# Loading the second attention's first query weights before the last rows of the first feed-forward are transposed

## The chip, the cores and the metric

The kernel runs on one core of one Trainium2 chip. The metric is device time in microseconds (us) of one execution, and the median of three executions is given. Five engines work side by side: TensorE (PE; its weight loads appear as PEld), VectorE (DVE), ScalarE (ACT), GpSimd (POOL) and SyncE (SP), which here issues nearly all transfers between the chip's main memory and its on-chip memory. Each engine works through its own instructions in order; semaphores hold an instruction back until what it needs is there.

## The reference

A trunk of two layers works on a sequence of 1024 rows of 1024 numbers. The first layer mixes rows with latent attention, the second with differential attention. A normalisation follows each mixer, then a gated feed-forward and a normalisation. The place of the change is the seam between the first layer's feed-forward and the second layer's mixer:

```python
def _swiglu(x, w_gu, w_down):
    gate, up = jnp.split(x @ w_gu, 2, axis=-1)
    return (jax.nn.silu(gate) * up) @ w_down

def _diff_mixer(x, w_in, ...):
    h = x @ w_in
    q, k, v = jnp.split(h, [qk_w, 2 * qk_w], axis=-1)
    ...

for i in range(DEPTH):
    ...
    h = _layernorm(ALPHA * h + mix, ln_mix_g[i], ln_mix_b[i])
    h = _layernorm(ALPHA * h + _swiglu(h, ffn_w_gu[i], ffn_w_down[i]), ln_ffn_g[i], ln_ffn_b[i])
```

## The kernel before

Every float32 product is made of three products of rounded parts: an operand is split into a high part (ACT casts it, line 519 or 136) and a low part (the operand less its high part, line 520 or 137, on DVE or POOL), and TensorE adds high by high, high by low and low by high.

The feed-forward's down projection saves multiplications by combining blocks of its operands (the h side and the w side) before the products. Its last product, called t4 here, runs over 11 steps j = 0 to 10. For each step an h block is split (tile op_h, low part on DVE) and a w block is built and split: DVE subtracts (line 865, rw_t less tt), ACT casts (op_w_t), POOL subtracts for the low part. Then TensorE adds twelve 128x512 matmuls into four banks named dw (line 889). The blocks come in three loads each: rh holds the h blocks, rw_t the w blocks of steps 0-3, 4-7 and 8-10. There are two buffers for rh, so the third rh load, and behind it on SP the third rw_t load, is asked for when the first rh block has been used up by step 3.

This is how TensorE takes one step of t4 (its order, step 3, with the engines that it waits for; the numbers behind the tiles are buffer numbers):

```order
L889 MATMUL dw_0_9091<-op_w_t_3_9877,op_h_4_3_9873 128x512 [waits Activation_49]
L889 MATMUL dw_1_9092<-op_w_t_3_9877,op_h_4_3_9873 128x512
L889 MATMUL dw_2_9093<-op_w_t_3_9877,op_h_4_3_9873 128x512
L889 MATMUL dw_3_9094<-op_w_t_3_9877,op_h_4_3_9873 128x512
L889 MATMUL dw_0_9091<-op_w_t_3_9877,op_h_4_3_9873 128x512 [waits Pool_49]
L889 MATMUL dw_0_9091<-op_w_t_3_9877,op_h_4_3_9873 128x512 [waits DVE_49]
L889 MATMUL dw_1_9092<-op_w_t_3_9877,op_h_4_3_9873 128x512 x2
```

Four matmuls need high parts alone, the fifth needs POOL's low part of w, the sixth DVE's low part of h. This stands the same before and after the change.

After t4 the rows are normalised (`layer_norm`): DVE centres a row block (line 176), ACT squares it (line 170), POOL takes a power (line 181, tile rs_f), DVE scales (line 184), and TensorE transposes it (line 148, tile xTp_f). The second mixer's first products follow: values (tile bv, weights wbv) and, for head 0, queries (tile bp, weights wb0_0).

`load_w` loads one weight block and splits it; it is where the change acts:

```python
raw = wp.tile([P, 1024], F32, tag="wr", bufs=2, name=f"r_{name}")
nc.sync.dma_start(raw[:, :cols], src)                                        # line 132
hi = wp.tile([P, 1024], F32R, tag="wh", name=f"h_{name}")
lo = wp.tile([P, 1024], F32R, tag="wl", name=f"l_{name}")
A.copy(hi[:, :cols], raw[:, :cols])                                          # line 136
j = (eng or G).tensor_tensor(lo[:, :cols], raw[:, :cols], f32(hi[:, :cols]), ALU.subtract)   # 137
```

The raw buffers (tag wr) are two and are taken in turn. `next_x` runs when the stage t4 has been written down and loads the value weights; `proj_b` loads query and key weights when a head first asks for them. `behind(i, j)` puts instruction i behind j in the order, without a semaphore. The order on each engine is set at build time by a scheduler with priorities, so where an instruction is written does not alone say where it stands.

Of the kernel before, what the change touches and what calls it, by code (L numbers as in the profile page):

```python
# [42 lines left out]
def trunk(  # L43
# [63 lines left out]
    def f32(t):  # L107
        return t.bitcast(F32)
# [7 lines left out]
    def ps_m(name):  # L116
        return ps.tile([P, 512], F32, tag="m", bufs=ps_bufs[1], name=name)
# [10 lines left out]
    def load_w(src, cols, name, hi=None, lo=None, eng=None, raw=None, ins=False):  # L128

        if raw is None:  # L130
            raw = wp.tile([P, 1024], F32, tag="wr", bufs=2, name=f"r_{name}")
        nc.sync.dma_start(raw[:, :cols], src)
        if hi is None:
            hi = wp.tile([P, 1024], F32R, tag="wh", name=f"h_{name}")
            lo = wp.tile([P, 1024], F32R, tag="wl", name=f"l_{name}")
        A.copy(hi[:, :cols], raw[:, :cols])
        j = (eng or G).tensor_tensor(lo[:, :cols], raw[:, :cols], f32(hi[:, :cols]), ALU.subtract)
        return (hi, lo, j.ins) if ins else (hi, lo)

    def mm3(ps_out, pairs):  # L140
        n = len(pairs)
        for i, (lh, ll, rh, rl) in enumerate(pairs):
            T.matmul(ps_out, lh, rh, start=(i == 0), stop=False)  # L143
            T.matmul(ps_out, lh, rl, start=False, stop=False)  # L144
            T.matmul(ps_out, ll, rh, start=False, stop=(i == n - 1))  # L145
# [9 lines left out]
    def behind(i, j):  # L155

        tc.add_manual_dep(
            i, j.name,
            mybir.DependencyInfo(mybir.DependencyClass.NoSync, mybir.DependencyReason.DATA),
            reason="kept in program order",  # L160
        )
# [38 lines left out]
    def new_xT(pool, name):  # L200
        t = {
            (p, hf): pool.tile([P, KD, 512], F32R, tag=f"xT{p}{hf}", name=f"xT{p}{hf}_{name}")
            for hf in range(2) for p in range(2)
        }
        return [[t[p, hf] for hf in range(2)] for p in range(2)]
# [327 lines left out]
    def swap(side):  # L533
        return "left" if side == "right" else "right"

    def ffn(side, xo, xst, pending, layer, x_src, x_dst, lng, lnb, next_x, spare=()):


# [494 lines left out]
        else:  # L1033
# [3 lines left out]
            whole(y4, from_h(2, "4", ("o",)), t4(), False)  # L1037
            stx.close()
            new = next_x()
            with tc.high_priority(60):  # L1040
                for t in range(4, 8):
# [169 lines left out]
    with ast as st:  # L1211
# [6 lines left out]
        vt, qr, qn, kn, wts, lt, pts = {}, {}, {}, {}, {}, {}, {}  # L1218
# [125 lines left out]
    xst, wts = ExitStack(), {}  # L1344

    def next_x():
        pool = xst.enter_context(tc.tile_pool(name="xp0", bufs=1, side="right", reuse_waits="tile"))
        wts["v", 0] = [load_w(w_b_v[0, kh], 1024, f"wbv0_{kh}") for kh in range(2)]
        return new_xT(pool, "f0")

    xo, stacks = x_pools("m0", "right")
# [2 lines left out]
    def split_wo(h, c):  # L1354

        cs = slice(c * 512, c * 512 + 512)
        raw = wp.tile([P, 1024], F32, tag="wr", name=f"pwo{h}_{c}", bufs=2)[:, :512]
        nc.sync.dma_start(raw, w_o_b[h][:, cs])
        nc.sync.dma_start(wo_dr[h][:, :, cs], f32(op_unit(raw, V, f"pwo{h}_{c}")))

    xT, rest, normed = ffn(
        "left", xo, stacks, pending, 0, xs_dr[0], xs_dr[1], ln_ffn_g[0], ln_ffn_b[0], next_x,
        [lambda h=h, c=c: split_wo(h, c) for h in range(H) for c in range(2)],
    )
# [3 lines left out]
    with ExitStack() as st:  # L1368
# [11 lines left out]
        for ql in q_lo:  # L1380
            for mp in range(2):
                b = slice(64 - mp * 64, 128 - mp * 64)
                z = bb[b, :512]
                i = G.tensor_tensor(ql[b, mp * 512:mp * 512 + 512], z, z, ALU.subtract).ins
# [20 lines left out]

        def proj_b(h, which, hf):
            if (which, h) not in wts:
                *wts[which, h], i = load_w(w_b_qk[h, which], 1024, f"wb{h}_{which}", ins=True)
                if len(wts) == 2:
                    behind(i, normed[0][2])  # L1410
            wh, wl = wts[which, h]
            hs = slice(hf * 512, hf * 512 + 512)
            m = ps_m(f"bp{h}_{which}_{hf}")
            mm3(m, [(wh[:, k * P:k * P + P], wl[:, k * P:k * P + P], xT[0][hf][:, k, :], xT[1][hf][:, k, :])
                    for k in range(KD)])
            sc = float(2.0 ** (h + 1) / 8.0)
            if which == 0:
                j = 2 * h + (hf if h < H - 1 else 1 - hf)
                q2, ql = q_slot[h, hf] = q_hi[j % 3], q_lo[j % 3]
                for mp in range(2):  # L1420
                    a = slice(mp * 64, mp * 64 + 64)
                    b = slice(64 - mp * 64, 128 - mp * 64)
                    qh = q2[:, mp * 512:mp * 512 + 512]
                    A.activation(qh[a], m[a, :], AF.Copy, scale=sc)
                    V.scalar_tensor_tensor(
                        ql[a, mp * 512:mp * 512 + 512], m[a, :], sc, f32(qh[a]), ALU.mult, ALU.subtract
                    )
                    nc.gpsimd.dma_start(qh[b], qh[a])
            else:
                for mp in range(2):  # L1430
                    a = slice(mp * 64, mp * 64 + 64)
                    b = slice(64 - mp * 64, 128 - mp * 64)
                    k = kt[h % 2][:, mp]
                    A.copy(k[a, hs], m[a, :])
                    V.tensor_tensor(k[b, hs], m[a, :], f32(k[a, hs]), ALU.subtract)
# [74 lines left out]
        at(-1, first_values)  # L1510
        at(-1, rest[0])
        at(-1, proj_b, 0, 0, 1)
        for tb in range(4):
            for fn in rest[tb + 1:tb + 2]:
                at(-1, fn)
            at(-1, values_b, 0, tb)
        at(-1, proj_b, 0, 0, 0)
        at(-1, proj_b, 0, 1, 0)
        at(-1, proj_b, 0, 1, 1)
        at(-1, table)  # L1520
# [128 lines left out]
```

## Time and profile before

| what | us |
|---|---|
| median of 3 executions | 2256.71 |
| lowest and highest | 2256.47 and 2257.42 |
| the profiled execution | 2256.85 |
| its span in the trace | 2255.1 |
| TensorE busy in the span | 2235.1 |

The profile is of one execution. The span runs from the first to the last instruction, and the profiled execution's own time is 1.75 us longer. Times in the timelines count from the start of the span. In a timeline row the first number is the start, the second the time from the first start to the last end of the merged instructions, `x3` their count, and the bracket at the end says how long the engine was idle before and what ended that.

### The profile page before, as it was taken

How to read it: one execution, taken by the hardware profiler on the slowest of the kernel's cores; microseconds unless marked ns; L12 is line 12 of the kernel's file. 1: busy time of each engine (PE TensorE's matmuls, PEld its weight loads, DVE VectorE, ACT ScalarE, POOL GpSimd, SP SyncE). 2: the span in 40 equal slices, each digit the busy share in tenths (PEclk: the TensorE clock that was granted, in tenths of full speed). 3: DMA queues.
4: the chain of work that ended last, by engine and by line, in shares of the span. 5: the costliest groups of instructions: out<-in, count | busy, mean ns of one | idle time of the engine just before them, and what ended most of it. 6: DMA issues, size and time to landing. Idle time of an engine off the chain costs nothing.

```text
span 2255.1 us, 31061 instructions
## 1 busy us (share of the span) xinstructions
PE 2235.1 (99%) x11410; PEld 1911.9 (85%) x11410; DVE 1543.9 (68%) x2894; ACT 1014.0 (45%) x2097; POOL 773.5 (34%) x626
## 2 busy tenths in 40 slices
PE   9999999999999999999999999999999999999998
PEld 8899998888888888888989898988888888888886
DVE  5676765696666657767576666577787656658778
ACT  4455664352333334444465656455432333334444
POOL 2232341114434440456432424222014444430551
PEclk9999999999999999999999999999999999999999
DMA  5010125334535338454310212063344232238453
GB/s 204 14 35 32 42 71 187 141 130 146 181 126 201 121 131 327 177 201 150 103 44 32 64 34 68 24 224 131 121 148 163 82 110 101 102 112 331 160 183 149
DMA packets 105545, 287.76 MB, mean 128 GB/s; under 512 B 7968, under 2 KB 30112, under 8 KB 94896
## 3 DMA queue, kind: packets, MB, share of 16 engines
q1 hardware_dynamic: 101552, 277.44, 34.6%
q0 software_dynamic: 3840, 8.33, 1.4%
q8 instruction: 90, 1.47, 0.3%
q14 instruction: 63, 0.52, 0.1%
HBM read 204.47 MB, written 77.07 MB: 125 GB/s over the span
## 4 chain that ended last, share of the span: by engine, by line
PE 96%; DVE 2%; DMA 1%; ACT 1%; issue 1%; POOL 0%; SPq 0%; DVEq 0%; POOLq 0%; ACTq 0%
PE gb L563 16%; PE gc L563 11%; PE ga L563 10%; PE dw L889 8%; PE dx L889 5%; PE zp_a L431 4%; PE s_a L220 3%; PE s_b L220 3%; PE dv L889 3%; PE dy L889 3%; PE bp L145 3%; PE bp L143 3%; PE bp L144 3%; PE o_a L263 2%; PE o_b L263 2%; PE hq L1142 2%
## 5 line engine op out<-in xcount | busy, mean ns | idle before, releaser
L519 ACT CAST op_g<-gr 128x512 fp32r<-128x512 f32 x240 | 146.8, 621 | 377.9 <-PE gb L563 185.8
L520 POOL TENSOR_TENSOR op_g<-gr,op_g 128x512 fp32r<-128x512 f32 x104 | 144.9, 1398 | 253.8 <-ACT op_g L519 141.6
L520 DVE TENSOR_TENSOR op_h<-rh,op_h 128x512 fp32r<-128x512 f32 x152 | 140.1, 948 | 51.1 <-ACT op_h L519 51.1
L563 PE MATMUL ga<-xh_m,op_g 128*128 128x512 f32 x512 | 168.2, 389 | 0.0
L889 PE MATMUL dw<-op_w_t,op_h 128*128 128x512 f32 x660 | 151.2, 390 | 0.0
L519 ACT CAST op_h<-rh 128x512 fp32r<-128x512 f32 x152 | 91.9, 619 | 124.3 <-PE dx L889 32.6
L889 PEld LDWEIGHTS dw<-op_w_t,op_h 128*128 128x128 f32 x660 | 123.6, 188 | 25.8 <-DVE op_h L520 0.3
L228 ACT ACTIVATE l_b<-l_b,mx_b 128x256 f32<-128x256 f32 (+7 forms) x128 | 99.4, 777 | 74.8 <-DVE mx_b L223 72.9
L520 DVE TENSOR_TENSOR op_g<-gr,op_g 128x512 fp32r<-128x512 f32 x136 | 112.9, 833 | 17.1 <-ACT op_g L519 16.8
L520 POOL TENSOR_TENSOR op_w_b<-rw_b,op_w_b 128x512 fp32r<-128x512 f32 x44 | 64.7, 1493 | 172.1 <-ACT op_w_b L519 172.0
L1451 POOL TENSOR_SCALAR l_b<-l_b,rb,cst 128x128 f32<-128x128 f32 (+3 forms) x64 | 52.5, 821 | 200.5 <-DVE rb L1450 188.0
L889 PE MATMUL dx<-op_w_b,op_h 128*128 128x512 f32 x528 | 120.3, 389 | 0.0
L889 PEld LDWEIGHTS dx<-op_w_b,op_h 128*128 128x128 f32 x528 | 99.1, 188 | 20.6
L563 PE MATMUL gb<-t2h_f,op_g 128*128 128x512 f32 x352 | 115.4, 390 | 0.4 <-DVE op_g L520 0.4
L563 PE MATMUL gc<-t1h_f,op_g 128*128 128x512 f32 x352 | 115.6, 389 | 0.0
L563 PE MATMUL gb<-t4h_f,op_g 128*128 128x512 f32 x352 | 115.5, 389 | 0.0
L563 PE MATMUL gc<-b22h_f,op_g 128*128 128x512 f32 x352 | 115.4, 389 | 0.0
L563 PE MATMUL gb<-t3h_f,op_g 128*128 128x512 f32 x352 | 115.2, 389 | 0.0
L563 PEld LDWEIGHTS ga<-xh_m,op_g 128*128 128x128 f32 x512 | 96.1, 188 | 19.9
L520 POOL TENSOR_TENSOR op_g<-s,op_g 128x512 fp32r<-128x512 f32 x40 | 55.2, 1381 | 166.5 <-ACT op_g L519 158.6
L143 PE MATMUL bp<-xT_f,h_wb 128*128 128x512 f32 x256 | 101.8, 398 | 0.0
L144 PE MATMUL bp<-xT_f,h_wb 128*128 128x512 f32 x256 | 101.6, 397 | 0.0
(389 smaller groups left out, 6689.5 us busy)
## 6 DMA issues: line engine op xcount, KB each, us to landing
gr<-in_w_gu SPq DMA_DIRECT2D x44, 1024.0 KB, 6.8
rh<-h_dr SPq DMA_DIRECT2D x28, 1024.0 KB, 4.8
h_dr<-sh SPq DMA_DIRECT2D x22, 1024.0 KB, 5.0
h_dr<-hp SPq DMA_DIRECT2D x22, 768.0 KB, 4.1
tt<-in_w_dn SPq DMA_DIRECT2D x22, 512.0 KB, 8.8
rh<-h_dr SPq DMA_DIRECT2D x12, 768.0 KB, 4.4
wo_dr<-op_pwo SPq DMA_DIRECT2D x16, 512.0 KB, 3.3
z<-xs_dr SPq DMA_DIRECT2D x16, 512.0 KB, 11.1
```

Of the source, the lines that this page charges most:

```text
L143: T.matmul(ps_out, lh, rh, start=(i == 0), stop=False)
L144: T.matmul(ps_out, lh, rl, start=False, stop=False)
L145: T.matmul(ps_out, ll, rh, start=False, stop=(i == n - 1))
L220: T.matmul(s[:, :w], lh, rh[:, ks], start=(j == 0), stop=(j == len(q_pass) - 1))
L228: ends["exp"] = A.activation(l[:, :n], l[:, :n], AF.Exp, bias=mx, scale=-1.0, accum_out=sm).ins
L263: T.matmul(po[:, c], a, b[:, j % 2, c], start=st, stop=sp_, skip_group_check=True)
L431: T.matmul(m, a[:, h, :], self.wo[h][w][:, c], start=(start and h == heads[0] and a is oh and w == 0), stop=(stop and h == heads[-1] and a ...
L519: turns["cast"] = A.copy(hi, src).ins
L520: return eng.tensor_tensor(lo, src, f32(hi), ALU.subtract).ins
L563: T.matmul(o, w[:, a, k * P:(k + 1) * P], x[b][:, k, :], start=(first and k == 0 and (a, b) == (0, 0)), stop=(k == 3 and a == 1), skip_gro ...
L889: T.matmul(o, h[:, a, c], w[:, b_], start=(first and (a, b_) == (0, 0)), stop=(last and a == 1), skip_group_check=True,).ins for a, b_ in ...
L1451: G.tensor_scalar(l1[:, :n], l1[:, :n], r[:, 1:2], nlam, ALU.mult, ALU.mult)
```

## The change

The first query weights of head 0 (wb0_0) are loaded and split in `next_x`, right after the value weights, and no longer in `proj_b`. With that the line that put their low part behind the power of the first normalised row block (`normed[0][2]`, tile rs_f_0) goes away.

```diff
     def next_x():
         pool = xst.enter_context(tc.tile_pool(name="xp0", bufs=1, side="right", reuse_waits="tile"))
         wts["v", 0] = [load_w(w_b_v[0, kh], 1024, f"wbv0_{kh}") for kh in range(2)]
+        wts[0, 0] = load_w(w_b_qk[0, 0], 1024, "wb0_0")
         return new_xT(pool, "f0")
...
         def proj_b(h, which, hf):
             if (which, h) not in wts:
-                *wts[which, h], i = load_w(w_b_qk[h, which], 1024, f"wb{h}_{which}", ins=True)
-                if len(wts) == 2:
-                    behind(i, normed[0][2])
+                wts[which, h] = load_w(w_b_qk[h, which], 1024, f"wb{h}_{which}")
             wh, wl = wts[which, h]
```

On POOL, in the stage t4, one piece of the difference between the two orders (l_wbv_1 is the low part of the second value weights, l_wb_0 the moved low part of the query weights):

```order
 L520 TENSOR_TENSOR op_w_t_1_9839<-rw_t_0_9817,op_w_t_1_9839 128x512
 L137 TENSOR_TENSOR l_wbv_1_10047<-r_wbv_1_10044,h_wbv_1_10046 128x1024
+L137 TENSOR_TENSOR l_wb_0_10053<-r_wb_0_10050,h_wb_0_10052 128x1024
 L520 TENSOR_TENSOR op_w_t_2_9858<-rw_t_0_9817,op_w_t_2_9858 128x512
 L520 TENSOR_TENSOR op_w_t_3_9877<-rw_t_0_9817,op_w_t_3_9877 128x512
```

The low part of wb0_0 now stands ahead of the low parts of t4's steps 2 to 10. Before, it stood behind the whole of t4, after the power of row block 0:

```order
L520 TENSOR_TENSOR op_w_t_10_10018<-rw_t_2_9977,op_w_t_10_10018 128x512
L181 TENSOR_TENSOR rs_f_0_10130<-ve_f_0_10128,cst 128x1
L137 TENSOR_TENSOR l_wb_0_10335<-r_wb_0_10332,h_wb_0_10334 128x1024
L181 TENSOR_TENSOR rs_f_1_10143<-ve_f_1_10141,cst 128x1
L181 TENSOR_TENSOR rs_f_2_10156<-ve_f_2_10154,cst 128x1
```

and that place is now empty. On ACT the cast moves in the same way, as one piece of the difference shows:

```order
 L136 CAST h_wbv_1_10046<-r_wbv_1_10044 128x1024
 L519 CAST op_h_4_2_9854<-rh_4_0_9812 128x512
+L136 CAST h_wb_0_10052<-r_wb_0_10050 128x1024
 L519 CAST op_w_t_2_9858<-rw_t_0_9817 128x512
 L519 CAST op_h_4_3_9873<-rh_4_0_9812 128x512
```

The cast now stands ahead of the casts of w step 2 and h step 3; before, it stood behind the casts of the transposed rows, after t4. On SP, before (xs_dr is the write of a normalised row block, bb a table of the second attention):

```order
L185 DMA xs_dr_98<-z_6_8613 128x1024
L185 DMA xs_dr_98<-z_7_8614 128x1024
L794 DMA rh_4_2_9972<-h_dr_2_5308 128x1536
L794 DMA rw_t_2_9977<-in_w_dn 128x3x512
L132 DMA r_wb_0_10332<-in_w_b_qk 128x1024
L1373 DMA bb<-in_c_bias_b 128x1024
L185 DMA xs_dr_98<-y_f_0_10110 128x1024
L132 DMA r_wb_1_10558<-in_w_b_qk 128x1024
```

and after:

```order
L185 DMA xs_dr_98<-z_6_8613 128x1024
L185 DMA xs_dr_98<-z_7_8614 128x1024
L132 DMA r_wb_0_10050<-in_w_b_qk 128x1024
L794 DMA rh_4_2_9972<-h_dr_2_5308 128x1536
L794 DMA rw_t_2_9977<-in_w_dn 128x3x512
L132 DMA r_wb_1_10558<-in_w_b_qk 128x1024
L1374 DMA bb<-in_c_bias_b 128x1024
```

The request for wb0_0 passes the third loads of t4, and the request for the key weights wb0_1 takes the place that it leaves. In the new order the request waits for the low part of the first value weights (the reader of the raw buffer that it now gets), and the next request, r_wb_1, for its own low part.

On DVE the order of instructions is the same before and after. In the stage t4 it holds the subtractions of w steps 2 to 7 in a row, and the low part of h step 3 behind them:

```order
L906 SCALAR_TENSOR_TENSOR z_3_8416,fs_3_8644<-z_3_8416,dw_3_9094 128x512
L865 TENSOR_TENSOR rw_t_0_9817<-rw_t_0_9817,tt_2_8377 128x512
L865 TENSOR_TENSOR rw_t_0_9817<-rw_t_0_9817,tt_3_8376 128x512
L865 TENSOR_TENSOR rw_t_1_9897<-rw_t_1_9897,tt_4_8375 128x512
L865 TENSOR_TENSOR rw_t_1_9897<-rw_t_1_9897,tt_5_8374 128x512
L865 TENSOR_TENSOR rw_t_1_9897<-rw_t_1_9897,tt_6_8373 128x512
L865 TENSOR_TENSOR rw_t_1_9897<-rw_t_1_9897,tt_7_8372 128x512
L520 TENSOR_TENSOR op_h_4_3_9873<-rh_4_0_9812,op_h_4_3_9873 128x512
L520 TENSOR_TENSOR op_h_4_4_9894<-rh_4_1_9892,op_h_4_4_9894 128x512
L520 TENSOR_TENSOR op_h_4_5_9915<-rh_4_1_9892,op_h_4_5_9915 128x512
L865 TENSOR_TENSOR rw_t_2_9977<-rw_t_2_9977,tt_8_8371 128x512
L520 TENSOR_TENSOR op_h_4_6_9934<-rh_4_1_9892,op_h_4_6_9934 128x512
```

Nothing moved there. On TensorE only the four transposes of the last row block's second half change place: two matmuls of t4 now stand between them, so TensorE goes over from transposes to matmuls twice more than before.

## The prediction

> **What bounds the kernel now.** I read the page first: how busy each engine is, then the chain that ended last.
>
> ```profile
> PE 2235.1 (99%) x11410; PEld 1911.9 (85%) x11410; DVE 1543.9 (68%) x2894; ACT 1014.0 (45%) x2097; POOL 773.5 (34%) x626
> ...
> PE 96%; DVE 2%; DMA 1%; ACT 1%; issue 1%; POOL 0%; SPq 0%; DVEq 0%; POOLq 0%; ACTq 0%
> ```
>
> TensorE works 99% of the span and is 96% of the chain, so an edit elsewhere counts only where it makes TensorE wait or spares it a wait. Next the busy time by stretch around the change: 1041 to 1072 us is the last product, t4; then come the normalisation and the first products of the second attention. Columns: length, then PE, PEld, DVE, ACT and POOL busy, clock, DMA share and GB/s.
>
> ```profile
> 1041.00:1049.40 8.40, 8.40 (x46) 7.07 (x45) 8.40 (x14) 2.30 (x5) 5.27 (x4) 1.00 0.01 2
> 1049.40:1072.00 22.60, 22.60 (x103) 18.71 (x102) 11.33 (x16) 11.40 (x21) 11.29 (x8) 1.00 0.28 96
> 1072.00:1082.00 10.00, 9.33 (x75) 8.86 (x74) 10.00 (x21) 6.55 (x15) 2.93 (x2) 1.00 0.13 50
> 1082.00:1130.00 48.00, 48.00 (x301) 43.35 (x300) 22.79 (x45) 21.27 (x41) 20.78 (x18) 1.00 0.39 117
> ```
>
> And who waited on TensorE from 1041 to 1130 us, the whole answer (total, times, longest):
>
> ```profile
> PE xTp_f L148 <- DVE y_f L184: 0.7, 1, 0.7
> ```
>
> TensorE never waits in t4, though DVE is full in its first 8.4 us. Its one wait is behind the scaling of row block 0 (line 184). At 1082 to 1130 us, where the query weights are used, it waits for nothing: wb0_0 is in time as it is.
>
> **What the change takes away.** DVE's rows at that wait, then POOL's, then TensorE's:
>
> ```profile
> 1078.68 2.74 DVE L184 SCALAR_TENSOR_TENSOR y_f<-y_f,rs_f,gb_f 128x1024 f32<-128x1024 f32 x1
> ...
> 1083.73 1.29 DVE L184 SCALAR_TENSOR_TENSOR y_f<-y_f,rs_f,gb_f 128x1024 f32<-128x1024 f32 x1
> ```
>
> ```profile
> 1077.92 2.42 POOL L137 TENSOR_TENSOR l_wb<-r_wb,h_wb 128x1024 fp32r<-128x1024 f32 x1
> ```
>
> ```profile
> 1080.52 0.28 PE L145 MATMUL bv<-h_wbv,xT_f 128*128 128x256 f32 x1
> 1081.47 0.66 PE L148 MATMUL xTp_f<-ident,y_f 128*128 128x128 f32 x4 [0.67 <-DVE y_f L184]
> 1081.88 0.36 PE L143 MATMUL bv<-h_wbv,xT_f 128*128 128x256 f32 x1
> 1082.09 0.28 PE L144 MATMUL bv<-l_wbv,xT_f 128*128 128x256 f32 x1
> ```
>
> Row block 0's scaling takes 2.74 us, row block 1's 1.29. During the first, POOL computes the low part of wb0_0 until 1080.34, and the scaling ends 1.08 us after that: it stood still. With that POOL instruction gone it ends at 1078.68 + 1.29 = 1079.97. TensorE could start the transposes 0.12 us (the spacing of the bv matmuls) after 1080.52, at 1080.64; it starts at 1081.47. So 0.83 us come back, the whole gap, with 0.67 us of slack on DVE. The ACT cast of wb0_0 (1.05 us) also leaves this stretch; ACT has 3.4 us free there and nobody waits for it, so that is worth nothing.
>
> The two extra turns from transposes to matmuls cost something: after transposes the next matmul comes 0.21 us later (1081.88 to 1082.09) and not 0.12. Two such turns: +0.18 us, just ahead of the first bv.
>
> **What the change adds in t4.** Here the question is what the POOL instruction does to DVE at its new place. First, how the two engines behave when both want to run there now, POOL's rows and then DVE's:
>
> ```profile
> 1035.14 1.28 POOL L520 TENSOR_TENSOR op_w_t<-rw_t,op_w_t 128x512 fp32r<-128x512 f32 x1
> 1036.38 3.38 POOL L137 TENSOR_TENSOR l_wbv<-r_wbv,h_wbv 128x1024 fp32r<-128x1024 f32 x1
> 1039.72 1.74 POOL L520 TENSOR_TENSOR op_w_t<-rw_t,op_w_t 128x512 fp32r<-128x512 f32 x1
> 1041.42 2.85 POOL L137 TENSOR_TENSOR l_wbv<-r_wbv,h_wbv 128x1024 fp32r<-128x1024 f32 x1
> 1045.63 1.55 POOL L520 TENSOR_TENSOR op_w_t<-rw_t,op_w_t 128x512 fp32r<-128x512 f32 x1 [1.36 <-ACT op_w_t L519]
> ```
>
> ```profile
> 1035.20 2.30 DVE L184 SCALAR_TENSOR_TENSOR z<-z,rs_f,fb 128x1024 f32<-128x1024 f32 x1 [0.45 <-POOL rs_f L181]
> 1037.43 2.88 DVE L520 TENSOR_TENSOR op_h<-rh,op_h 128x512 fp32r<-128x512 f32 x1
> ```
>
> Of DVE's six subtractions of w steps 2 to 7 the first, all six merged, and the fourth:
>
> ```profile
> 1043.76 1.06 DVE L865 TENSOR_TENSOR rw_t<-rw_t,tt 128x512 f32<-128x512 f32 x1
> 1043.76 5.17 DVE L865 TENSOR_TENSOR rw_t<-rw_t,tt 128x512 f32<-128x512 f32 x6
> 1045.95 1.78 DVE L865 TENSOR_TENSOR rw_t<-rw_t,tt 128x512 f32<-128x512 f32 x1
> ```
>
> Order the ends: POOL 1036.42, DVE 1037.50, POOL 1039.76, DVE 1040.31, POOL 1041.46. They take turns, one instruction each, and the one that waits does no work: a 128x512 instruction of DVE ends 0.55 us after POOL's, POOL's ends 1.15 us after DVE's, and POOL's 128x1024 ends 2.26 us after DVE's. The row at 1045.95 is the same: it is still there at 1047.73, 0.55 us after POOL's 1047.18.
>
> [...]
>
> When does the moved work arrive? SP's rows, and how long the block asked for at 1049.92 takes to land:
>
> ```profile
> 1031.66 6.19 SPq L185 DMA_DIRECT2D xs_dr<-z  x2
> 1049.56 0.32 SPq L794 DMA_DIRECT2D rh<-h_dr  x1
> 1049.92 0.43 SPq L794 DMA_DIRECT2D rw_t<-in_w_dn  x1
> ```
>
> ```profile
> rw_t<-in_w_dn SPq DMA_DIRECT2D x1, 768.0 KB, 6.6
> ```
>
> And a later load of the moved kind, its request, cast and subtraction:
>
> ```profile
> 1110.13 0.33 SPq L132 DMA_DIRECT2D r_wb<-in_w_b_qk  x1
> ```
>
> ```profile
> 1113.71 1.05 ACT L136 CAST h_wb<-r_wb 128x1024 fp32r<-128x1024 f32 x1 [4.43 <-DMA r_wb<-in_w_b_qk]
> ```
>
> ```profile
> 1114.84 2.40 POOL L137 TENSOR_TENSOR l_wb<-r_wb,h_wb 128x1024 fp32r<-128x1024 f32 x1 [2.39 <-ACT h_wb L136]
> ```
>
> SP is free at 1037.85, but the raw buffer only when POOL's row of 1036.38 ends, at 1039.76: request at 1039.8. From request to cast 3.58 us, from cast to POOL's start 1.13: cast at 1043.4, ahead of the w cast of step 2, and POOL's subtraction at 1044.5, with the transfer engines nearly idle (share 0.01). DVE's first subtraction (step 2) ends at 1044.82 as before, and then the turns go on: wb0_0's low part 1047.08, DVE step 3 1047.63, w2 low 1048.78, step 4 1049.33, w3 low 1050.48, step 5 1051.03, w4 low 1052.18, step 6 1052.73. Now DVE's step 7, POOL's w5 low and DVE's low part of h3 follow in one order or the other; either way h3's low part ends near 1055.04. Before, POOL had gaps in which DVE got several instructions done. Who needs these? TensorE's row, then the low parts of h3 and w5 and the third w block's first subtraction as they run now:
>
> ```profile
> 1049.43 22.95 PE L889 MATMUL dw<-op_w_t,op_h 128*128 128x512 f32 x100
> ```
>
> ```profile
> 1048.85 0.68 DVE L520 TENSOR_TENSOR op_h<-rh,op_h 128x512 fp32r<-128x512 f32 x1
> ...
> 1052.83 1.29 POOL L520 TENSOR_TENSOR op_w_t<-rw_t,op_w_t 128x512 fp32r<-128x512 f32 x1 [0.43 <-ACT op_w_t L519]
> ...
> 1056.56 0.78 DVE L865 TENSOR_TENSOR rw_t<-rw_t,tt 128x512 f32<-128x512 f32 x1 [3.60 <-DMA rw_t<-in_w_dn]
> ```
>
> The matmul at 1049.43 is the fifth of step 2; w2's low part (1048.78) is in time by 0.65 us. A matmul takes 0.228 us (22.95 over 100, less the last one's tail), a step of twelve 2.73. So the sixth matmul of step 3, which needs h3's low part, is due at 1049.43 + 2.73 + 0.23 + 0.08 (a turn from transposes) = 1052.47. Today that part is there at 1049.53, 2.9 us early; then it would be 2.6 us late, and TensorE stands for **2.6 us**.
>
> What is late next: the third rh load waits for that same low part (1049.53, request at 1049.56), the third w block right behind it. They are asked for at 1055.1 and 1055.4, and after 6.6 us, as now, the w block is there at 1062.0. DVE's order has its first subtraction ahead of the low part of h6, which ends near 1062.0 + 0.7 + 0.6 = 1063.3; TensorE, itself 2.6 late, needs it at 1052.5 + 3 x 2.73 + 2.6 = 1063.3. I take 0.1 us there and 0.2 for step 7, whose low part has two more turns with POOL ahead of it: **0.3 us**.
>
> The request for wb0_1 takes wb0_0's old place on SP at the same distance from the third w block, so the traffic there stays; wb0_1 comes about 30 us earlier and its cast waits for its buffer as before: nothing.
>
> Sum: 2.6 + 0.3 + 0.18 - 0.83 = **+2.3 us**. The profiled execution took 2256.85, 0.14 above the median; on the median 2256.71 this gives **2259.0**. Bounds of the unknown term, the stall in t4: below, none (DVE keeps its 2.9 us of slack), above 5.1 (2.9 and the 2.2 at which the third rival passes 0.2%). The reading in turns is nearest, because every row above where both engines want to run fits it to 0.05 us.
>
> **The rivals.** First, the stall does not come: if a busy POOL only slows DVE, then the six subtractions, 4.1 us at 0.68 each, took 5.17 beside 2.1 us of POOL (to 1044.27, and 1.55), so they lose some 0.5 us per us of POOL; 2.4 us more of it cost 1.3 of the 2.9 us slack. Then the 0.83 stays: 2256.71 - 0.65 = 2256.1. The 2.74 us row speaks against it.
>
> Second, wb0_0 lands later than 1044.4: ACT's cast then holds up the cast of w2, and POOL comes when DVE is two or three subtractions further on. TensorE waits 0.8 to 2 us for w2's low part instead, and less for h3: 2257.5 to 2258.5. An idle fabric speaks against it.
>
> Third, and on the slower side: the third w block lands late. Each us beyond 6.6 is a us of TensorE at step 6, since the slack there is used up; from 8.8 us on the sum passes 0.2% (4.5 us, about what a measurement of this kernel tells from no change): 2261.2 or more. Three loads are in flight then, as now, which speaks against more than 6.6.
>
> **How the numbers follow.** Forecast 0.62, first rival 0.22, second 0.08, third 0.08. The range: the forecast's own is 2257.9 to 2260.5; down to 2255.8 it takes in the first rival, whose 2256.1 carries the 0.3 of scatter seen in the runs. Only the third rival lies beyond 0.2%; 0.02 I leave for a gain that I do not see. So faster 0.02, within 0.2% 0.90, slower 0.08.
>
> **What the profile after would show.** Right: POOL's l_wb at about 1044.5, DVE's line 865 rows each waiting a POOL instruction, a TensorE wait on op_h (line 520) near 1052.5 of 2 to 3 us, the scaling of row block 0 at 1.3 us and no wait of xTp_f for it. Wrong: no TensorE wait in t4, or one on POOL's op_w_t; a third w block that lands later than 6.6 us after its request.

## The result and the profile after

The changed kernel takes 2259.74 us (median of 22 executions, 2257.55 to 2261.72); the kernel before, run beside it on the same chip, 2256.68 (22 executions, 2255.03 to 2257.42). The ratio is 1.0015, 95% interval 1.0009 to 1.002: 3.1 us slower, within the 0.2% that the prediction set as its bound. The profiled execution took 2259.6, with a span of 2257.8. One of the ten executions of e4 below took 9820.35 us, for a cause that no trace shows, and e4's median there is that of the other nine.

Busy time by stretch, columns as before (length, PE, PEld, DVE, ACT, POOL, clock, DMA share, GB/s):

```profile
1041.00:1049.40 8.40, 8.40 (x46) 7.07 (x44) 8.40 (x13) 3.24 (x5) 8.06 (x5) 1.00 0.19 60
1049.40:1075.00 25.60, 23.18 (x102) 18.41 (x101) 16.68 (x19) 11.59 (x22) 11.38 (x8) 1.00 0.25 84
1075.00:1085.00 10.00, 10.00 (x81) 9.65 (x80) 9.56 (x22) 5.62 (x14) 0.55 (x1) 1.00 0.25 95
```

POOL is now full in t4's first 8.4 us (8.06, before 5.27). TensorE lacks 2.42 us in the second stretch, where it lacked nothing, and is full in the third, where it lacked 0.67. Who waited on TensorE from 1041 to 1130 us, the whole answer:

```profile
PE dw L889 <- DVE op_h L520: 2.4, 1, 2.4
```

Behind it stand DVE's subtractions for w steps 3, 4 and 7 and the low part of h3 (the h block of step 3; w2 is the w block of step 2, and so on), and POOL's rows beside them:

```profile
1044.87 2.89 DVE L865 TENSOR_TENSOR rw_t<-rw_t,tt 128x512 f32<-128x512 f32 x1
1047.68 1.77 DVE L865 TENSOR_TENSOR rw_t<-rw_t,tt 128x512 f32<-128x512 f32 x1
...
1052.77 0.68 DVE L865 TENSOR_TENSOR rw_t<-rw_t,tt 128x512 f32<-128x512 f32 x1
1053.38 1.74 DVE L520 TENSOR_TENSOR op_h<-rh,op_h 128x512 fp32r<-128x512 f32 x1
```

```profile
1044.59 2.62 POOL L137 TENSOR_TENSOR l_wb<-r_wb,h_wb 128x1024 fp32r<-128x1024 f32 x1 [0.19 <-ACT h_wb L136]
1047.17 5.13 POOL L520 TENSOR_TENSOR op_w_t<-rw_t,op_w_t 128x512 fp32r<-128x512 f32 x3
1052.93 1.64 POOL L520 TENSOR_TENSOR op_w_t<-rw_t,op_w_t 128x512 fp32r<-128x512 f32 x1 [0.63 <-ACT op_w_t L519]
```

A subtraction of DVE alone took 0.68 here (1052.77). Step 3's took 2.89, because POOL's l_wb ran until 1047.21 and DVE ended 0.55 later; step 4's took 1.77 behind POOL's next. So it goes on in turns to the low part of h3 at 1055.12. TensorE's rows show what that cost:

```profile
1049.53 3.22 PE L889 MATMUL dw<-op_w_t,op_h 128*128 128x512 f32 x13
1055.17 1.20 PE L889 MATMUL dw<-op_w_t,op_h 128*128 128x512 f32 x4 [2.42 <-DVE op_h L520]
```

The third loads and ACT's casts of h blocks, which follow TensorE's steps, show what is late next:

```profile
1055.15 0.32 SPq L794 DMA_DIRECT2D rh<-h_dr  x1
1055.52 0.43 SPq L794 DMA_DIRECT2D rw_t<-in_w_dn  x1
```

```profile
rw_t<-in_w_dn SPq DMA_DIRECT2D x1, 768.0 KB, 6.6
```

```profile
1059.81 0.62 ACT L519 CAST op_h<-rh 128x512 fp32r<-128x512 f32 x1 [1.58 <-PE dw L889]
1062.53 0.62 ACT L519 CAST op_h<-rh 128x512 fp32r<-128x512 f32 x1 [1.58 <-PE dw L889]
1065.44 0.62 ACT L519 CAST op_h<-rh 128x512 fp32r<-128x512 f32 x1 [1.77 <-PE dw L889]
1068.36 0.62 ACT L519 CAST op_h<-rh 128x512 fp32r<-128x512 f32 x1 [1.77 <-PE dw L889]
```

A step takes 2.72; the two behind the third w block take 2.91 and 2.92, so 0.39 more. And at the normalisation, DVE's and TensorE's rows:

```profile
1075.17 0.69 DVE L1048 SCALAR_TENSOR_TENSOR y_f<-z,dw 128x512 f32<-128x512 f32 x1 [2.67 <-PE dw L889]
...
1081.87 1.27 DVE L184 SCALAR_TENSOR_TENSOR y_f<-y_f,rs_f,gb_f 128x1024 f32<-128x1024 f32 x1
```

```profile
1083.87 0.60 PE L148 MATMUL xTp_f<-ident,y_f 128*128 128x128 f32 x4
```

The scaling of row block 0 is back at 1.27 us and TensorE no longer waits for it. The first row that needs a finished bank of t4 (line 1048) is the measure that I use from here on: **the stretch** from DVE's first subtraction of step 2 (line 865) to its first line 1048. Before, that row reads:

```profile
1071.95 0.69 DVE L1048 SCALAR_TENSOR_TENSOR y_f<-z,dw 128x512 f32<-128x512 f32 x1 [2.66 <-PE dw L889]
```

Before, the stretch is 1071.95 - 1043.76 = 28.19 us; after, 1075.17 - 1043.88 = 31.29, so 3.10 more. From line 1048 to the transposes of row block 0 it was 1081.47 - 1071.95 = 9.52 and is 8.70: 0.82 less. The net is 2.3 us. It repeats well between traces: the six kernels that leave t4 without a wait and DVE's work in it unchanged (before, e1, e2, e3, e5, e9) have a stretch of 28.19 or 28.20, where the times of the 22 executions of before scatter over 2.4 us.

### The profile page after: what moved, and what is told of

Read it like the earlier page. It is cut to its first block, busy times and chain, and to the rows that moved or that the text cites. A ratio compares the mean times of both kernels' runs of the same rounds, so it can differ in the third digit from the quotient of the medians.

```text
span 2257.8 us, 31065 instructions
## 1 busy us (share of the span) xinstructions
PE 2235.8 (99%) x11410; PEld 1912.6 (85%) x11410; DVE 1546.5 (68%) x2894; ACT 1014.7 (45%) x2097; POOL 775.7 (34%) x626
## 4 chain that ended last, share of the span: by engine, by line
PE 94%; DVE 3%; DMA 1%; issue 1%; ACT 1%; POOL 0%; SPq 0%; DVEq 0%; POOLq 0%; ACTq 0%
PE gb L563 16%; PE gc L563 10%; PE ga L563 10%; PE dw L889 6%; PE dx L889 4%; PE zp_a L431 4%; PE s_a L220 4%; PE s_b L220 3%; PE dv L889 3%; PE bp L145 3%; PE bp L143 3%; PE bp L144 3%; PE dy L889 3%; PE o_a L263 2%; PE o_b L263 2%; PE hq L1142 2%
```

## The experiments

All twelve, with the stretch, TensorE's wait in t4, the scaling of row block 0, and the medians of the kernel and of before in the same set:

| run | stretch | wait in t4 | scaling | median | before |
|---|---|---|---|---|---|
| before | 28.19 | none | 2.74 | | |
| after | 31.29 | 2.4 | 1.27 | 2259.74 | 2256.68 |
| e1, low part behind the first row power | 28.19 | none | 2.72 | 2256.23 | 2256.53 |
| e3, low part at t4's end | 28.19 | none | 1.27 | 2255.57 | 2256.53 |
| e7, h3's low part first | 28.32 | none | 1.28 | 2256.00 | 2256.53 |
| e8, low part twice | 35.79 | 0.9 and 3.4 | 1.27 | 2262.85 | 2256.53 |
| e2, no pin alone | 28.20 | none | 1.28 | 2256.53 | 2255.92 |
| e4, low part on DVE | 28.61 | none | 1.27 | 2255.81 | 2255.92 |
| e5, one fill | 28.19 | none | 1.27 | 2255.27 | 2255.92 |
| e6, half early | 29.15 | 0.2 | 1.27 | 2256.95 | 2255.92 |
| e9, three fills | 28.19 | none | 1.28 | 2255.69 | 2256.30 |
| e10, two halves | 32.50 | 2.4 | 1.28 | 2259.24 | 2256.30 |
| a1, after again | 31.37 | 2.4 | 1.28 | 2258.75 | 2256.20 |
| a2, after again | 32.51 | 2.4 | 1.28 | 2259.37 | 2256.20 |

a1 and a2 are one execution each. Only after, e8 and e10 differ from before by more than their intervals; the rest is read from the stretch.

**Early load, late low part (e1).** Request and cast stay early; only the low part is written in `proj_b` again, behind `normed[0][2]`.

```diff
+    nc.sync.dma_start(raw, w_b_qk[0, 0]); A.copy(hi, raw)                 # next_x
...
+    behind(G.tensor_tensor(lo, raw, f32(hi), ALU.subtract).ins, normed[0][2])   # proj_b
```

> Request and cast of wb0_0 stay early, only POOL's low part goes back behind the first row power. Theory (in t4 POOL and DVE take turns, and POOL's early l_wb pushes the low part of h3 back by a turn of 2.8 us): no wait of TensorE on op_h in t4, the scaling of row block 0 back at 2.7 us with the wait of 0.7 behind it, the two extra turns of transposes left: 2256.9, within 0.3 us of before. First rival (the early request, cast or transfer costs the time): the t4 wait of 2.4 us stays, and the 0.8 us gained is lost again: 2260.5. Second rival (POOL is merely busier and w low parts come late): as the theory.

```profile
1043.03 5.17 DVE L865 TENSOR_TENSOR rw_t<-rw_t,tt 128x512 f32<-128x512 f32 x6
...
1071.22 0.69 DVE L1048 SCALAR_TENSOR_TENSOR y_f<-z,dw 128x512 f32<-128x512 f32 x1 [2.66 <-PE dw L889]
```

The six subtractions take 5.17 again, as before to the hundredth, and the stretch is 28.19. The ratio to before is 0.9999 (0.9991 to 1.0008). The request, the transfer and the cast cost nothing; the first rival of the experiments (that one of these costs the time) falls, and all of the loss is POOL's one instruction.

**The low part at t4's end (e3).**

```diff
-        wts[0, 0] = load_w(w_b_qk[0, 0], 1024, "wb0_0")
+        *wts[0, 0], i = load_w(w_b_qk[0, 0], 1024, "wb0_0", ins=True)
+        behind(i, turns["last"])
```

> Request and cast of wb0_0 stay early, POOL's low part goes behind the last low part of t4's w, at about 1067.7 us, where DVE reads PSUM and then idles. Theory: no wait of TensorE in t4 and a scaling of 1.3 us with no wait behind it: 0.65 us less than before, 2256.1. First rival (early request, cast or transfer): the t4 wait of 2.4 stays, 2259.7. Second rival (busy POOL): 2256.1 as well.

POOL's row, then DVE's:

```profile
1068.24 2.43 POOL L137 TENSOR_TENSOR l_wb<-r_wb,h_wb 128x1024 fp32r<-128x1024 f32 x1
```

```profile
1044.38 5.17 DVE L865 TENSOR_TENSOR rw_t<-rw_t,tt 128x512 f32<-128x512 f32 x6
...
1079.27 1.27 DVE L184 SCALAR_TENSOR_TENSOR y_f<-y_f,rs_f,gb_f 128x1024 f32<-128x1024 f32 x1
```

Here the instruction meets no DVE work that it holds up: both costs are gone, the stretch is 28.19 and the transposes of row block 0 come 8.70 us after line 1048. In the trace this is 0.8 us better than before; the time, 0.9997 (0.9988 to 1.0006), cannot tell it from before.

**DVE's order instead (e7).** The low part stays early on POOL; DVE takes h3's low part ahead of its subtractions of steps 5 to 7. (Lines 867 and 1052 of this kernel are lines 865 and 1048 of the others.)

```diff
+                    if next_x is not None and 4 < j < 8:
+                        behind(i, ends["h3"])        # the low part of op_h step 3
```

> As after, but DVE's low part of h3 goes ahead of its subtractions of w steps 5 to 7. Theory: l_wb stays early, and h3's low part still ends near 1051.1, ahead of the 1052.5 at which TensorE wants it; then 0 to 0.5 us of wait at h4, the third loads are asked for at about 1051.2, the 0.8 us stays gained: 2256.1 to 2256.6. First rival (early request, cast or transfer) and second rival (busy POOL makes w low parts late): the wait stays whatever DVE's order is, 2259 to 2260.

```profile
1043.35 5.59 DVE L867 TENSOR_TENSOR rw_t<-rw_t,tt 128x512 f32<-128x512 f32 x3
1048.86 1.78 DVE L520 TENSOR_TENSOR op_h<-rh,op_h 128x512 fp32r<-128x512 f32 x1
```

POOL and DVE take turns as in after, but h3's low part ends at 1050.64, and TensorE does not wait: stretch 28.32 (0.13 more), ratio 0.9998 (0.9989 to 1.0008). So the turns cost TensorE time only because h3's low part stands behind all six subtractions.

**Twice the work (e8).** The low part is computed twice over.

```diff
+        for _ in range(2):
+            G.tensor_tensor(lo, raw, f32(hi), ALU.subtract)
```

> As after, but POOL computes wb0_0's low part twice over, one after the other (same values). Theory: one more pair of turns, 2.26 + 0.55 = 2.8 us: TensorE's waits in t4 grow from 2.4 to about 5.2, part of it now on w2's low part (about 2.1) and the rest on h3's (about 3.2); 2262.5. First rival (request, cast, transfer): 2259.7 as after. Pro rata slowing of DVE by a busy POOL instead of turns: the wait grows by 1.3, 2261.0.

TensorE's waits from 1041 to 1130 us, then its stretches there:

```profile
PE dw L889 <- DVE op_h L520: 3.4, 1, 3.4
PE dw L889 <- POOL op_w_t L520: 0.9, 1, 0.9
```

```profile
1049.00:1055.20 6.20, 2.86 (x12) 1.79 (x10) 6.20 (x4) 2.27 (x4) 6.20 (x4) 1.00 0.00 0
1055.20:1062.00 6.80, 5.83 (x14) 4.59 (x15) 2.12 (x3) 1.14 (x2) 1.59 (x2) 0.50 0.64 216
1062.00:1066.00 4.00, 4.00 (x19) 3.31 (x18) 2.85 (x4) 1.14 (x2) 1.30 (x2) 1.00 0.39 157
```

The time, 2262.85, is near the 2262.5 expected, but not by its working, so that is luck. The waits add up to 4.3 us and not 5.2 (the second l_wb stood behind w2's low part in POOL's order, so w2 was in time and w3 waited 0.9); and the stretch grew by 7.6, because TensorE's granted clock was 0.50 for 6.8 us, from inside the second wait on; TensorE came back at 1056.17. That I had not foreseen; it is taken up in a1 and a2.

**The pin alone (e2).** Before, without the pin.

```diff
-                if len(wts) == 2:
-                    behind(i, normed[0][2])
```

> The kernel before with the pin alone taken away: load, cast and low part of wb0_0 stay where they are emitted, and POOL now has the low part ahead of the first row power (rs_f_0) and not behind it. Theory: nothing changes in t4 (no wait of TensorE there); POOL's l_wb begins when the cast ends, near 1077.2 us, and holds rs_f_0 back until about 1079.7; the scaling of row block 0 then takes 1.3 us and ends near 1081.5 as before: wait of xTp_f 0.7 to 1.1 us, 2256.7 to 2257.1. Were the pin's loss the cause of the 2.4 us in t4, this run would show them: 2259.

TensorE's waits from 1041 to 1130 us, the whole answer, and DVE's row:

```profile
PE xTp_f L148 <- DVE y_f L184: 0.8, 1, 0.8
```

```profile
1080.02 1.28 DVE L184 SCALAR_TENSOR_TENSOR y_f<-y_f,rs_f,gb_f 128x1024 f32<-128x1024 f32 x1 [1.51 <-POOL rs_f L181]
```

As expected: t4 is untouched (28.20), POOL takes l_wb first, the first row power ends late, and the scaling, 1.28 us now, begins at 1080.02. TensorE waits 0.8 instead of 0.7. The pin is worth about nothing, and its loss is not what costs the time in t4.

**The low part on DVE (e4).**

```diff
+        wts[0, 0] = load_w(w_b_qk[0, 0], 1024, "wb0_0", eng=V)
```

> As after, but DVE computes wb0_0's low part, between its subtractions of w steps 2 to 7 and the low part of h3; POOL has no work of it. Theory (turns with POOL): DVE's six subtractions take 5.2 us again as before, its own l_wb 1.3 us and at most one turn of 1.15 with POOL, so h3's low part ends between 1050.9 and 1052.1, ahead of 1052.5: no wait in t4, scaling 1.3 us, 2256.1. If instead any work added to DVE or POOL in t4 costs its length there, TensorE waits 1 to 2 us: 2257.5 to 2258.

```profile
1048.03 1.21 DVE L137 TENSOR_TENSOR l_wb<-r_wb,h_wb 128x1024 fp32r<-128x1024 f32 x1
```

On DVE the same work takes 1.21 us. It moves h3's low part by about its own length and one turn with POOL: that ends at 1050.94, 8.00 us after the first subtraction, before 5.77. That is still in time; no wait in t4, ratio 1.000 (0.999 to 1.001). The stretch is 0.42 longer: the third loads are asked for 2 us later, and two steps pay 0.2 each, as in after.

**Work that reads nothing (e5, e9).** The low part as in e3; at its early place POOL fills the tile with zeros, once (e5) or three times (e9).

```diff
+        for _ in range(3):                           # e5: once
+            G.memset(f32(lo), 0.0)
+        behind(G.tensor_tensor(lo, raw, f32(hi), ALU.subtract).ins, turns["last"])
```

> The low part of wb0_0 goes behind t4's last w low part as in the run that put it there, and at its early place POOL fills the same 128x1024 tile with zeros (overwritten later): work of POOL that writes SBUF and reads nothing. Theory, if turns come from reads only: DVE's subtractions run at 0.7 to 1.1 us beside the fill, no wait on h3 in t4, 2256.1. If any POOL instruction on SBUF takes the turn: a wait of up to 2.4 us on op_h, in the measure of the fill's length (a fill of 2.4 us: 2259.0). If POOL's being busy matters and not DVE's standing still: the same, but the wait is on POOL's op_w_t.

> As the run with one fill of zeros, but with three of them, 0.96 us each in that run: 2.9 us of POOL's time at the early place of l_wb, longer than l_wb's own 2.26, that write and read nothing; the low part itself behind t4's last w low part. Theory (only POOL work that reads SBUF makes DVE stand): the subtractions beside the fills take 0.7 us each, w2's low part ends near 1047.5 and so in time, no wait of TensorE in t4; 2256.1. If it is POOL's being busy that counts (its gaps closed, the w low parts pushed back): TensorE waits 1 us or more on op_w_t or op_h; 2257 or more.

POOL's row and DVE's in e9:

```profile
1044.51 2.98 POOL L1355 MEMSET l_wb<- 128x1024 f32 x3
```

```profile
1044.05 4.07 DVE L865 TENSOR_TENSOR rw_t<-rw_t,tt 128x512 f32<-128x512 f32 x6
```

POOL is busy for 2.98 us, longer than with l_wb (2.62 in after). DVE's first subtraction takes 1.06, behind the low part of the value weights as in before, and the other five take 0.68 each; the six are faster than before (5.17), since w2's low part no longer falls among them. No wait. e5's single fill, 0.96 us, shows the same at a smaller dose (stretch 28.19, no wait). What makes DVE stand still here is not a busy POOL but POOL's subtraction, which reads two tiles: beside it a subtraction of DVE took 1.77 to 2.89 us in after, beside the fills 0.68. Whether reading one tile would do was not tried.

**Half of it early (e6), and the whole in two halves (e10).**

```diff
+        G.tensor_tensor(lo[:, :512], raw[:, :512], f32(hi[:, :512]), ALU.subtract)
+        # columns 512 on: e6 behind turns["last"], e10 right here
```

> As after, but only the first 512 columns of wb0_0's low part are computed early; the other 512 behind t4's last w low part. Theory (turns): POOL's turn is 1.15 us and not 2.26, so h3's low part comes 1.1 us sooner and TensorE's wait is 2.4 - 1.1 = 1.3 us: 2258.6. Pro rata slowing of DVE (0.5 us per us of POOL): 0.6 less, 1.8 us, 2259.1. First rival (request, cast, transfer), which the runs so far speak against: 2.4 us.

> As after, with wb0_0's low part early in two instructions of 512 columns in place of one of 1024: the same work, one more handover to DVE. Turns of one instruction each: DVE gets a subtraction between the halves, h3's low part ends 0 to 1.2 us sooner, TensorE's wait in t4 is 1.2 to 2.4 us: 2258.5 to 2259.7. If the run with half the work gained because POOL's gaps between its w low parts came back, and not by the turns, the wait here stays at 2.4, since POOL's work is the same.

e6, DVE's subtractions, then POOL's half and its next two rows:

```profile
1043.56 7.37 DVE L865 TENSOR_TENSOR rw_t<-rw_t,tt 128x512 f32<-128x512 f32 x6
```

```profile
1044.30 1.47 POOL L1354 TENSOR_TENSOR l_wb<-r_wb,h_wb 128x512 fp32r<-128x512 f32 x1 [0.23 <-ACT h_wb L1353]
1045.73 1.74 POOL L520 TENSOR_TENSOR op_w_t<-rw_t,op_w_t 128x512 fp32r<-128x512 f32 x1
1048.75 1.63 POOL L520 TENSOR_TENSOR op_w_t<-rw_t,op_w_t 128x512 fp32r<-128x512 f32 x1 [1.28 <-ACT op_w_t L519]
```

I expected 1.3 us of wait and 2258.6; there were 0.2 and 2256.95. The half saves 1.1 us of turn and another 1.1, because POOL now reaches w3's low part before its cast is done and idles 1.28 us, in which DVE takes two subtractions unhindered. In after that gap was closed. e10, DVE and POOL:

```profile
1042.89 9.58 DVE L865 TENSOR_TENSOR rw_t<-rw_t,tt 128x512 f32<-128x512 f32 x6
```

```profile
1043.72 3.09 POOL L1355 TENSOR_TENSOR l_wb<-r_wb,h_wb 128x512 fp32r<-128x512 f32 x2 [0.31 <-ACT h_wb L1353]
1046.77 6.82 POOL L520 TENSOR_TENSOR op_w_t<-rw_t,op_w_t 128x512 fp32r<-128x512 f32 x4
```

The same work in two pieces gives DVE one more turn, but POOL's 0.63 us gap ahead of w5's low part is gone, and the subtractions take 9.58 (after: 9.57). The wait is 2.4 again, ratio 1.0014 (1.0004 to 1.0023). Both readings allowed a wait of 2.4, so it does not decide between them; the rows do, since DVE's subtractions of steps 3 to 7 take one turn of 1.77 to 1.79 us each.

**The changed kernel twice more (a1, a2).** e10 has after's wait but a stretch 1.2 us longer, with the clock at 0.50 for 3.4 us behind the wait. Does that happen in the changed kernel itself?

> The changed kernel unaltered, another profiled execution. The profile after had the clock at 1.00 all through t4, and its stall and what follows add up to 2.3 us, while the medians lie 3.1 apart. If TensorE's pause of 2.4 us makes the granted clock fall to a half in some executions (as it did behind the pause of 2.4 us of the run with two halves, for 3.4 us), such a profile has 32.5 us from DVE's first line 865 of step 2 to its first line 1048, and a time near 2260.5; one without it has 31.3 us and a time near 2259.3. If the clock has no part in it, it is 1.00 here too and the interval 31.3 whatever the time.

> As the run before it, a third profiled execution of the changed kernel: 31.3 us and a clock of 1.00 in t4, or 32.5 us and a stretch of about 3.4 us at a clock of 0.50 behind the wait on h3's low part.

The window from 1055.70 to 1059.10, with TensorE back at work, in a1 and then in a2:

```profile
1055.70:1059.10 3.40, 3.40 (x17) 2.78 (x16) 0.18 (x1) 1.14 (x2) 1.21 (x1) 1.00 0.81 272
```

```profile
1055.70:1059.10 3.40, 3.40 (x10) 2.62 (x9) 0.00 (x0) 1.14 (x2) 1.28 (x1) 0.50 0.90 305
```

It does, in one of them: ten matmuls where a1 ran seventeen. a2's stretch, from the start of the first row below to that of the last, is 32.51, a1's 31.37, both as expected:

```profile
1043.03 9.56 DVE L865 TENSOR_TENSOR rw_t<-rw_t,tt 128x512 f32<-128x512 f32 x6
...
1075.54 0.69 DVE L1048 SCALAR_TENSOR_TENSOR y_f<-z,dw 128x512 f32<-128x512 f32 x1 [2.66 <-PE dw L889]
```

The times, 2259.37 and 2258.75, stand in the expected order, but below the expected 2260.5 and 2259.3, and 0.6 apart instead of 1.2. Most of that lies ahead of the stretch, which begins 0.38 us sooner in a2 than in a1 (1043.41).

## Why the prediction was right

The forecast was 2259.0, the median is 2259.74. Point by point, by its own steps:

- **When the moved work arrives**: request 1039.8, cast 1043.4, POOL at 1044.5 were forecast; they came at 1039.90, 1043.45 and 1044.59, in a trace that ran 0.12 us late at the first subtraction of step 2 (1043.88, before 1043.76). Right.
- **Turns of POOL and DVE**: right. The forecast had h3's low part end at 1055.04; it ended at 1055.12, in the trace that ran 0.1 late. The rows of steps 3 to 6 each waited for a POOL instruction (2.89 us and three of some 1.77); step 7's did not, it fell into a gap of POOL and h3's low part took the turn. The prediction had left that order open. e9 and e7 show the two halves of the reason: POOL's fills, which read nothing, did not stop DVE (0.68 us a subtraction in e9), and h3's place behind the turns is what costs time (with h3 ahead no wait, in e7).
- **The stall, 2.6 us**: 2.42 of idle time in the trace, and 2.7 by the starts, which is how the forecast counted: thirteen matmuls from 1049.53 at 0.228 put the next at 1052.49, and it started at 1055.17.
- **What is late next, 0.3**: 0.39; the third w block took the same 6.6 us to land, so the third rival did not come.
- **Two extra turns, +0.18**: not seen. The transposes of row block 0 start 8.70 us after line 1048; without the old wait it would have been 1080.64 - 1071.95 = 8.69 before.
- **The gain of 0.83**: 0.82, all of it.
- **The sum, +2.3**: 3.10 - 0.82 = 2.3 in the trace. The stall and what is late next came out 0.1 larger each and the turns 0.18 smaller; that these errors cancel is luck, the mechanism is not.

The first rival (a busy POOL slows DVE pro rata, 2256.1) falls with e9 and with the rows at 1.77 for each turn; the second (a late wb0_0) with the cast that was in time.

The medians lie 3.1 apart and not 2.3. The interval of the ratio, 1.0009 to 1.002, is 2.0 to 4.5 us and holds 2.3 as well, so the 0.8 may be scatter. Executions in which the clock falls could also make it up: in a2 the stretch is 1.1 longer than in a1, and two such executions in every three would do. How many there are was not counted, so this stays open.

No variant is measurably faster than before. By the traces e3, e5 and e9, which all have the low part at t4's end, are the best, 0.8 us ahead of before and 3 ahead of after.

## What to carry to other kernels

Before work is moved to an engine that "has time", look whether its instructions stop another engine's, and which one stands last in that engine's order: 2.4 us of POOL work (2.43 in e3) took 4.4 us from DVE here (9.57 for the six subtractions, before 5.17), since it also closed the gaps in which DVE had run free. A place behind t4's last low part of w (e3), where DVE had no such work in hand, cost nothing in t4 (stretch 28.19), half the work (e6) a third (29.15), and another order on the engine that is held up (e7) repaired it without moving anything (28.32).

## What was not expected of the hardware

In three of the five profiles in which TensorE paused for 2.4 us or more in t4, the pause cost more than its length, since the granted clock fell to 0.50. In a2 and e10 TensorE had resumed at 1054.31 and 1054.19 after 2.4 us, and the clock fell at 1055.7 and 1055.1, for 3.4 us; in e8 it fell at 1055.2, inside the second of two waits that add up to 4.3 us, and stayed down for 6.8 us, twice as long. In after and a1 the same pause of 2.4 us left it at 1.00. Why the same pause is charged in one execution and not in the next, no trace shows. How little TensorE did in and around the pause does not tell them apart: in the 3.4 us that end at the fall it was busy for 1.39 us in a2 and 1.01 in e10, and in as long a stretch of after, with the whole pause in it and the clock at 1.00, for 0.99 (the second number of each row; a2, e10, after):

```profile
1052.29:1055.70 3.41, 1.39 (x6) 1.17 (x7) 3.17 (x4) 0.00 (x0) 1.42 (x1) 1.00 0.11 14
```

```profile
1051.70:1055.10 3.40, 1.01 (x5) 0.79 (x5) 3.40 (x4) 0.20 (x1) 1.82 (x2) 1.00 0.00 0
```

```profile
1052.29:1055.70 3.41, 0.99 (x5) 0.52 (x4) 3.41 (x5) 0.56 (x2) 1.65 (x2) 1.00 0.00 0
```
